# The feed forward of a hybrid step in two phases through DRAM, its first product as seven block products

## The chip, the cores and the metric

The kernel runs on one core of one Trainium2 chip. The metric is device microseconds of one execution; the profile is one execution of the same program, recorded by the hardware profiler. TensorE (PE) multiplies matrices, VectorE (DVE) and ScalarE (ACT) do elementwise work and read PE's result banks, GpSimd (POOL) does small elementwise work and issues DMA transfers, SyncE (SP) issues DMA transfers.

## The reference, cut to what matters

```python
D_MODEL, D_FF, SEQ, DEC_SEQ = 1024, 4096, 128, 2048
# layer, same weights for 128 context and 2048 latent tokens
mix = concatenate([o_a, o_b, o_c], axis=-1) @ w_out
x = x + gate1 * mix
h = rmsnorm(x, norm2_g) * (1 + scale2) + shift2
x = x + gate2 * (square(relu(h @ w_ff1)) @ w_ff2)
y = rmsnorm(x, final_g)
```

w_out is 1024 x 1024, w_ff1 is 1024 x 4096, w_ff2 is 4096 x 1024, all fp32. The 2176 tokens are 17 tiles of 128: tile 0 holds the context, tiles 1 to 16 the latents.

## The kernel before, in words

Every product of fp32 operands is made of three matmuls: each operand is split into a high part (a rounding copy, ACT) and a low part (the operand less the high part, DVE or POOL), and mm3 adds high x high, high x low and low x high. A matmul takes 128 rows of contraction, 128 rows of output and up to 512 columns.

Three parts run one after the other: the attention and convolution groups, the output projection (its first rounding copy at 709 us) and the feed forward (from 944 us).

The output projection (out_proj, L752) goes through the tiles from 16 down to 0, 48 matmuls of 512 columns each. For a tile, the concatenated groups are loaded (mt, from mix_d), rounded on ACT (L771, hi) and subtracted on POOL (L772, lo). When its products are done, `done` applies gate and residual on DVE (L780, L781), stores x1 (L783, POOL's queue), squares on ACT, and gets the norm's factor by DVE (L156), POOL (L157) and ACT (L787). Four transposes per half and four ACT activations then give h2; these steps (h2_half) are woven into the next tile's products, behind 12 of its 16 units and behind the last. h2 is split and kept in SBUF for tiles 8 to 0, and stored to DRAM for 16 to 9.

The feed forward takes the tiles in two groups, GA (8 to 0) and GB (16 to 9). For a group it goes through 16 chunks of two feature tiles; in a chunk, through blocks of three tiles. ff1 makes z for a block (384 columns, 256 in GB's last block; 16 units of 3 matmuls), ACT applies relu, DVE squares and splits (L1194, L168). ff2 multiplies with w_ff2, 512 columns at a time, and DVE adds each result bank to a tile's sum in SBUF (L1222). GA's last chunk applies gate, residual and last norm woven between GB's first units; for GB, the gate is in w_ff2 already (L1259) and the residual starts the sum. The second group loads its h2 at the switch by POOL (L1284). Each group loads and splits both weights anew.

PE runs in the order of the code. The order of the instructions on ACT, DVE, POOL and SP is set by a scheduler when the kernel is built; each of them runs its list in order and stops at an instruction whose semaphore is not there.

## Time and profile before

| | |
|---|---|
| time, 3 runs | 2467.24, 2467.26 and 2470.92 us, median 2467.26 |
| profiled execution, first to last instruction | 2465.8 us |
| PE busy | 2405.0 us, 98% |
| DVE, ACT, POOL busy | 1505.7, 852.7 and 370.4 us |
| DMA | 259.30 MB, mean 105 GB/s |

The profiled execution's span leaves about 1.5 us of the runs' median to what lies around it. A row of the page has an engine's busy time; the time line has single instructions and the idle time in front of them with the instruction that ended it; the groups by line have mean durations. L lines are those of the kernel before. PE's matmul rows have modelled ends that overlap the next row's start, so a matmul's pace is read from the starts of two neighbouring rows.

### The profile page before, as it was taken

How to read it: one execution, taken by the hardware profiler on the slowest of the kernel's cores; microseconds unless marked ns; L12 is line 12 of the kernel's file. 1: busy time of each engine (PE TensorE's matmuls, PEld its weight loads, DVE VectorE, ACT ScalarE, POOL GpSimd, SP SyncE). 2: the span in 40 equal slices, each digit the busy share in tenths (PEclk: the TensorE clock that was granted, in tenths of full speed). 3: DMA queues.
4: the chain of work that ended last, by engine and by line, in shares of the span. 5: the costliest groups of instructions: out<-in, count | busy, mean ns of one | idle time of the engine just before them, and what ended most of it. 6: DMA issues, size and time to landing. Idle time of an engine off the chain costs nothing.

```text
span 2465.8 us, 34981 instructions
## 1 busy us (share of the span) xinstructions
PE 2405.0 (98%) x13906; PEld 2106.4 (85%) x13906; DVE 1505.7 (61%) x2674; ACT 852.7 (35%) x1792; POOL 370.4 (15%) x469
## 2 busy tenths in 40 slices
PE   7999999999999999999999999999999999999998
PEld 5788887777777878999999999999899999999997
DVE  5887845877888865444444444445955555545555
ACT  4666664333346675221212121212322222212212
POOL 2332325444424330000000000002100000000000
PEclk9999999999999999999999999999999999999999
DMA  8655635333354543111111111118821111111101
GB/s 284 230 198 197 220 107 182 122 127 126 126 178 172 207 164 120 43 50 36 52 35 41 46 46 41 35 52 154 263 81 42 51 52 52 38 48 52 52 18 69
DMA packets 162547, 259.30 MB, mean 105 GB/s; under 512 B 10597, under 2 KB 103055, under 8 KB 157776
## 3 DMA queue, kind: packets, MB, share of 16 engines
q1 hardware_dynamic: 128304, 172.86, 22.4%
q0 software_dynamic: 34080, 84.21, 10.6%
q8 instruction: 109, 1.79, 0.3%
q14 instruction: 54, 0.44, 0.1%
HBM read 188.07 MB, written 68.96 MB: 104 GB/s over the span
## 4 chain that ended last, share of the span: by engine, by line
PE 66%; DVE 12%; issue 4%; POOL 3%; ACT 3%; DMA 1%; POOLq 0%; DVEq 0%; SPq 0%; ACTq 0%
PE z L122 35%; PE g L122 30%; DVE cacc L69 6%; DVE uv L69 1%; POOL mv L157 1%; PE g L125 1%; DVE w L781 1%; DVE w L69 1%; POOL s L157 1%; DVE w L1222 0%; ACT w L66 0%; DVE w L168 0%; ACT osq L1056 0%; POOL ssq L157 0%; ACT uv L66 0%
## 5 line engine op out<-in xcount | busy, mean ns | idle before, releaser
L122 PE MATMUL g<-w,xp 128*128 128x512 f32 x3264 | 761.3, 391 | 4.3 <-DVE w L1222 4.3
L122 PEld LDWEIGHTS g<-w,xp 128*128 128x128 f32 x3264 | 611.3, 188 | 129.3 <-DVE w L1222 5.6
L122 PE MATMUL z<-w,hb 128*128 128x512 f32 (+1 forms) x3062 | 704.5, 377 | 4.6 <-ACT w L167 2.3
L122 PEld LDWEIGHTS z<-w,hb 128*128 128x128 f32 x3062 | 524.6, 190 | 105.0 <-issue 4.8
L122 PE MATMUL z<-ab,w 128*128 128x384 f32 x3072 | 544.8, 335 | 0.0
L122 PEld LDWEIGHTS z<-ab,w 128*128 128x128 f32 x3072 | 535.8, 188 | 4.9
L1222 DVE TENSOR_TENSOR w<-g,w 128x512 f32<-128x512 f32 x526 | 360.5, 690 | 191.8 <-PE g L122 190.5
L66 ACT ACTIVATE rl<-z 128x384 f32<-128x384 f32 (+1 forms) x192 | 90.5, 472 | 706.4 <-PE z L122 706.4
L1194 DVE TENSOR_TENSOR rl<-rl 128x384 f32<-128x384 f32 (+1 forms) x192 | 102.6, 534 | 342.0 <-ACT rl L66 342.0
L167 ACT CAST w<-raw 128x1024 fp32r<-128x1024 f32 x148 | 151.7, 1048 | 312.3 <-PE z L122 160.7
L168 DVE TENSOR_TENSOR w<-raw,w 128x1024 fp32r<-128x1024 f32 x147 | 179.8, 1235 | 122.1 <-ACT w L167 87.9
L122 PE MATMUL z<-h2c,w 128*128 128x384 f32 (+1 forms) x1536 | 232.1, 311 | 0.0
L122 PEld LDWEIGHTS z<-h2c,w 128*128 128x128 f32 x1536 | 229.4, 188 | 2.5
L69 DVE SCALAR_TENSOR_TENSOR cacc<-xp,wd,cacc 128x512 f32<-128x512 f32 (+2 forms) x360 | 231.3, 694 | 0.0
L157 POOL TENSOR_TENSOR ssq<-ssq,mhalf 128x1 f32<-128x1 f32 x51 | 38.5, 756 | 746.6 <-DVE ssq L156 738.7
L167 ACT CAST xp<-rl 128x384 fp32r<-128x384 f32 (+1 forms) x192 | 95.2, 496 | 128.0 <-DVE rl L1194 125.5
L168 DVE TENSOR_TENSOR xp<-rl,xp 128x384 fp32r<-128x384 f32 (+1 forms) x192 | 102.3, 533 | 51.8 <-ACT xp L167 51.8
L1284 POOL DMA_DIRECT2D ab<-h_d x12 | 10.6, 901 | 754.2 <-PE z L122 754.2
L69 DVE SCALAR_TENSOR_TENSOR cacc<-raw,sc,cacc 128x512 f32<-128x512 f32 x112 | 85.0, 796 | 0.3
L66 ACT ACTIVATE hc<-g,sh,s 128x128 f32<-128x128 f32 x128 | 50.3, 457 | 39.9 <-PE g L125 22.9
L66 ACT ACTIVATE w<-g,modc,s 128x128 f32<-128x128 f32 x136 | 51.8, 460 | 18.5 <-PE g L125 18.5
L1032 POOL TENSOR_TENSOR r<-fs,r 64x512 f32<-64x512 f32 x31 | 43.8, 1412 | 3.1 <-DMA r<-ss_d 0.7
(228 smaller groups left out, 1804.7 us busy)
## 6 DMA issues: line engine op xcount, KB each, us to landing
raw<-in_w_ff_dram SPq DMA_DIRECT2D x128, 512.0 KB
raw<-in_w_mod_dram SPq DMA_DIRECT2D x32, 512.0 KB
hb<-hT_d POOLq DMA_DIRECT2D x15, 1024.0 KB, 5.8
hT_d<-hb POOLq DMA_DIRECT2D x13, 1024.0 KB, 7.0
ss_d<-ss POOLq DMA_DIRECT2D x34, 256.0 KB, 4.0
r<-ss_d SPq DMA_DIRECT2D x34, 256.0 KB
x_d<-w POOLq DMA_DIRECT2D x17, 512.0 KB, 4.4
out_dram<-w SPq DMA_DIRECT2D x34, 256.0 KB
```

The costliest lines, as they stand in the source:

```text
L66: return S.activation(out=out, in_=in_, func=func, scale=scale, bias=bias, **kw)
L69: return V.scalar_tensor_tensor(out=out, in0=in0, scalar=scalar, in1=in1, op0=op0, op1=op1)
L122: tc.keep_in_program_order(T.matmul(out, lhsT, rhs, start=start, stop=stop))
L125: tc.keep_in_program_order(T.transpose(out, in_, ident if idn is None else idn))
L157: G.tensor_tensor(out=out, in0=out, in1=mhalf[:, 0:out.shape[-1]], op=ALU.pow)
L167: order(S.copy(out=hi, in_=src))
L168: order(V.tensor_tensor(out=lo, in0=src, in1=hi.bitcast(F32), op=ALU.subtract))
L781: V.tensor_tensor(out=x1[:, fs], in0=tmp[:, fs], in1=x1[:, fs], op=ALU.add)
L1032: G.tensor_tensor(out=r[64:128].rearrange("p (h v) -> p h v", h=H), in0=f, in1=r[64:128].rearrange("p (h v) -> p h v", h=H), op=ALU.add)
L1194: V.tensor_tensor(out=rl[:, 0:n], in0=rl[:, 0:n], in1=rl[:, 0:n], op=ALU.mult)
L1222: V.tensor_tensor(out=y[:, hs], in0=py, in1=y[:, hs], op=ALU.add)
L1284: st.dma_start(out=h2[1, b][a][:, :, jj * P:(jj + 1) * P], in_=h2_d[grp[3 * b + jj]][:, a])
```

## The change

The feed forward is no longer taken in chunks of both products. First h @ w_ff1 is made for all tokens and its squared relu stored to DRAM (f_d); then the second product runs over all 17 tiles in one pass.

For the first product the latent tiles are two groups g of eight (16 to 9, 8 to 1). A group's activations and a pair of feature tiles form a 2 x 2 by 2 x 2 block product: contraction halves of 512, token halves (even and odd tiles, 4 tiles, 512 columns), two feature tiles. It is made with seven block products and sums (Strassen, in Winograd's form) instead of eight. A unit (g, i), of which there are 32, is 7 products of 4 contraction tiles of 3 matmuls, 84 matmuls of 512 columns. Four of the products share result bank za, two zc, one gb; ACT and DVE read the partial sums on the way (ff1_units, `after`). The four left operands beside the plain weights come from four DVE sums per unit, and are split; the weights are loaded per unit, once for each g. The seven right operands come from h2: out_proj makes them per pair of an even and an odd tile with four DVE subtractions (h2_pair) and stores them to tb_d; 14 blocks of 512 KB per group are loaded back on POOL's queue (L1176) and split in place on ACT and DVE (L1169, L1170). The context tile has its own 24 matmuls of 256 columns per feature pair, beside g = 0.

For the second product, 8 chunks of four feature tiles; in each, blocks of four tiles and one block with the context. It has the same 3264 matmuls of 512 columns. F is reloaded (SP) and split in place, w_ff2 is loaded once. The first chunk is copied out by ACT, the other seven added by DVE (L1405). The last chunk applies gate, residual, square and last norm to each tile (finish, L1372 to L1376, L160, L161).

In out_proj, tiles below 16 take their loaded and split inputs from a new pool (T, 18 buffers), which later holds right operands and the sums. Its code is otherwise as before; lines are shifted (L771 is L767 now, L772 is L768, L780 is L777, L783 is L780, L787 is L784, L157 is L161).

```diff
         cq.finish(t)
-        if t > 2:
+        if t == NT - 1:
             hu, mt = hunit()
             mh, ml = hu[:, 0], hu[:, 1]
         else:
-            # the units hold the last block of the feed forward by now
-            mt, mh = raw(), xp_tile()[:, 0:D].bitcast(F32R)
-            ml = wtile() if t == 1 else xp_tile()[:, 0:D].bitcast(F32R)
+            mt, mh, ml = tunit(F32), tunit(), tunit()
         ld.dma_start(out=mt, in_=mix_d[t].rearrange("p k t -> p (k t)"))
         S.copy(out=mh, in_=mt)
         G.tensor_tensor(out=ml, in0=mt, in1=mh.bitcast(F32), op=ALU.subtract)
         x1 = wtile(F32)
...
+            if t == 0:
+                split(hc[0][:, ks], hc[1][:, ks], hf[:, ks])
+            elif kq == 1:
+                h2_pair(t, hf)
         return units, [(12, lambda: h2_half(0)), (16, lambda: h2_half(1))]
+    def h2_pair(t, hf):
+        g, j = (NT - 1 - t) // 8, (NT - 1 - t) % 8 // 2
+        js = slice(j * P, (j + 1) * P)
+        dst = tb_d[g]
+        if t % 2 == 0:
+            keep[0] = hf
+            st.dma_start(out=dst[:, 0:2, :, js], in_=hf.rearrange("p (i k) t -> p i k t", i=2))
+            return
+        b11, b21, b12, b22 = keep[0][:, 0:4], keep[0][:, 4:8], hf[:, 0:4], hf[:, 4:8]
+        cb = [tunit(F32).rearrange("p (i k t) -> p i k t", i=2, k=4) for _ in range(2)]
+        V.tensor_tensor(out=cb[0][:, 1], in0=b12, in1=b11, op=ALU.subtract)
+        V.tensor_tensor(out=cb[0][:, 0], in0=b22, in1=cb[0][:, 1], op=ALU.subtract)
+        V.tensor_tensor(out=cb[1][:, 0], in0=b22, in1=b12, op=ALU.subtract)
+        V.tensor_tensor(out=cb[1][:, 1], in0=b21, in1=cb[0][:, 0], op=ALU.subtract)
+        st.dma_start(out=dst[:, 5, :, js], in_=b22)
+        st.dma_start(out=dst[:, 2:4, :, js], in_=cb[0])
+        for i in range(2):
+            st.dma_start(out=dst[:, 4 + 2 * i, :, js], in_=cb[1][:, i])
...
+    hbs.close()
+    tp.append(tps.enter_context(tc.tile_pool(name="tp", bufs=1, side="right", reuse_waits="tile")))
+    hc = []
     for t in range(NT - 2, -1, -1):
         units, nxt_late = out_proj(t)
-        items = late3 + ticks(16, RATE3)
         if t == 0:
-            items.append((4, lambda: load_ff1(0, 0)))
-        weave(units, items)
+            hc += [tunit().rearrange("p (k t) -> p k t", k=KD) for _ in range(2)]
+        weave(units, late3 + ticks(16, RATE3))
         late3 = nxt_late
+    wps.close()
...
+    def split_in_place(hi, lo):
+        S.copy(out=hi, in_=lo.bitcast(F32))
+        V.tensor_tensor(out=lo, in0=lo.bitcast(F32), in1=hi.bitcast(F32), op=ALU.subtract)
+    def right_operand(g, i, kk, dst):
+        unit = tunit if i < 4 else uunit
+        hi, lo = unit(), unit()
+        st.dma_start(out=lo.bitcast(F32).rearrange("p (k n) -> p k n", k=2), in_=tb_d[g][:, i, 2 * kk:2 * kk + 2])
+        split_in_place(hi, lo)
+        dst[i, kk] = (hi, lo)
...
+            a1, a2 = (rw[x].rearrange("p (k f n) -> p k f n", k=4, f=2) for x in range(2))
+            sf[r] = cacc()
+            s_ = sf[r].rearrange("p (k f n) -> p k f n", k=4, f=2)
+            if r == 0:
+                V.tensor_tensor(out=s_[:, :, 0], in0=a1[:, :, 1], in1=a2[:, :, 1], op=ALU.add)
+                V.tensor_tensor(out=s_[:, :, 1], in0=s_[:, :, 0], in1=a1[:, :, 0], op=ALU.subtract)
+            else:
+                s2_ = sf[0].rearrange("p (k f n) -> p k f n", k=4, f=2)[:, :, 1]
+                V.tensor_tensor(out=s_[:, :, 0], in0=a1[:, :, 0], in1=a1[:, :, 1], op=ALU.subtract)
+                V.tensor_tensor(out=s_[:, :, 1], in0=a2[:, :, 0], in1=s2_, op=ALU.subtract)
+        def mixed(r):
+            hi, lo = wunit(), wunit()
+            split(hi, lo, sf[r])
+            w[2 + r] = [x.rearrange("p (k f n) -> p k f n", k=4, f=2) for x in (hi, lo)]
+        return w, [lambda: load(0), lambda: load(1), lambda: plain(0), lambda: plain(1),
+                   lambda: sums(0), lambda: mixed(0), lambda: sums(1), lambda: mixed(1)]
...
+    LEFT = ((0, 0), (1, 0), (2, 1), (2, 0), (3, 0), (3, 1), (1, 1))
+    def ff1_units(g, i, w, tb):
+        za, zc, gb = zbank(), zbank(), gbank()
+        f0, f1 = xp_tile()[:, 0:D], xp_tile()[:, 0:D]
+        left, right = slice(0, 512), slice(512, 1024)
+        bank = (za, gb, za, zc, za, zc, za)
+        def square(x):
+            stt(x, x, 0.0, x, ALU.max, ALU.mult)
+        def after(p):
+            if p == 0:
+                S.copy(out=f0[:, left], in_=za)
+            elif p == 1:
+                V.tensor_tensor(out=f0[:, left], in0=f0[:, left], in1=gb, op=ALU.add)
+                square(f0[:, left])
+            elif p == 2:
+                S.copy(out=f0[:, right], in_=za)
+            elif p == 3:
+                S.copy(out=f1[:, right], in_=zc)
+            elif p == 4:
+                V.tensor_tensor(out=f1[:, right], in0=f1[:, right], in1=za, op=ALU.add)
+                square(f1[:, right])
+            elif p == 5:
+                V.tensor_tensor(out=f0[:, right], in0=f0[:, right], in1=zc, op=ALU.add)
+                square(f0[:, right])
+                st.dma_start(out=f_d[i][g][:, 0], in_=f0)
+            else:
+                act(f1[:, left], za, AF.Relu)
+                V.tensor_tensor(out=f1[:, left], in0=f1[:, left], in1=f1[:, left], op=ALU.mult)
+                st.dma_start(out=f_d[i][g][:, 1], in_=f1)
+        def unit(p, k):
+            r, f = LEFT[p]
+            th, tl = tb[p, k // 2]
+            ks = slice(k % 2 * 512, (k % 2 + 1) * 512)
+            mm3(bank[p], w[r][0][:, k, f], w[r][1][:, k, f], th[:, ks], tl[:, ks],
+                k == 0 and p in (0, 1, 3), k == 3, p != 1)
+            if k == 3:
+                after(p)
+        return [lambda p=p, k=k: unit(p, k) for p in range(7) for k in range(4)]
...
+    TB = [{}, {}]
+    ORDER = [(i, kk) for i in range(7) for kk in range(2)]
+    w, steps = left_operand(0)
...
+        f()
+    for i, kk in ORDER[8:]:
+        right_operand(0, i, kk, TB[0])
...
+    turn = None
+    w2_first = []
+    for g in range(2):
+        for i in range(NP):
+            units = ff1_units(g, i, w, TB[g])
...
+                items += [(12, late3[0][1]), (20, late3[1][1])]
+            if (g, i) != (1, NP - 1):
+                w, steps = left_operand((i + 1) % NP)
+                items += zip((0, 0.5, 5.5, 10.5, 13.5, 17.5, 18.5, 25.5), steps)
+            if (g, i) == (0, NP - 1):
+                items += [(4 * p + 4.5 + kk, lambda p=p, kk=kk: right_operand(1, p, kk, TB[1])) for p, kk in ORDER]
...
+    def load_f(c, b):
+        out = []
+        def step(p):
+            i = c * CF // 2 + p
+            hi, lo = uunit(), uunit()
+            n = 512 if b < 4 else P
+            lv = lo[:, 0:2 * n]
+            src_ = f_d[i][b // 2][:, :, b % 2 * 512:b % 2 * 512 + 512] if b < 4 else fc_d[i]
+            ld.dma_start(out=lv.bitcast(F32).rearrange("p (f n) -> p f n", f=2), in_=src_)
+            split_in_place(hi[:, 0:2 * n], lv)
+            out.append([x[:, 0:2 * n].rearrange("p (f n) -> p f n", f=2) for x in (hi, lo)])
...
+                mm3(py, fh[:, f % 2, js], fl[:, f % 2, js], w2[f][0][:, hs], w2[f][1][:, hs], f == 0, f == CF - 1)
+                if f < CF - 1:
+                    return
+                if c == 0:
+                    if h == 0:
+                        ya[t] = tunit(F32)
+                    S.copy(out=ya[t][:, hs], in_=py)
+                else:
+                    V.tensor_tensor(out=ya[t][:, hs], in0=py, in1=ya[t][:, hs], op=ALU.add)
+                if c == NC_ - 1:
+                    if h == 0:
+                        fin.append(finish(t, ya[t]))
+                    fin[0](h)
...
+        w2n = []
+        for b in range(5):
+            units = ff2_units(c, b, F, w2)
+            items = []
+            nb, ncx = (b + 1, c) if b < 4 else (0, c + 1)
+            if ncx < NC_:
+                F, steps = load_f(ncx, nb)
+                items += zip((3.5, 9.5) if b < 4 else (0, 1), steps)
+            if c + 1 < NC_ and b < 4:
+                items.append((14.5, lambda f=(c + 1) * CF + b: w2n.append(load_ff2(f))))
+            weave(units, items)
+        w2 = w2n
+    tps.close()
```

What stands on ACT in the middle of the output projection, before: L787 is a tile's last scaling (tile 10 and 9 here), L771 the rounding copy of a later tile's input (7 and 6).

```order
L787 ACTIVATE w<-w,ssq_8775 128x1024
L66 ACTIVATE w<-g,modc,s_4853 128x128 x4
L167 CAST ab<-w 128x512
L771 CAST hb<-hc 128x1024
L66 ACTIVATE w<-g,modc,s_4853 128x128 x4
L66 ACTIVATE w,ssq_8875<-w 128x1024
L167 CAST ab<-w 128x512
L787 ACTIVATE w<-w,ssq_8875 128x1024
L66 ACTIVATE w<-g,modc,s_4853 128x128 x4
L167 CAST ab<-w 128x512
L771 CAST hb<-hc 128x1024
```

After: L784 is the last scaling of tile 12, 11 and 10, L767 the rounding copies of tiles 11 and 10, then of 9 and 8.

```order
L64 ACTIVATE w<-g,modc,s_4886 128x128
L784 ACTIVATE w<-w,ssq_8604 128x1024
L767 CAST T<-T 128x1024 x2
L64 ACTIVATE w<-g,modc,s_4886 128x128 x7
L64 ACTIVATE w,ssq_8709<-w 128x1024
L64 ACTIVATE w<-g,modc,s_4886 128x128
L784 ACTIVATE w<-w,ssq_8709 128x1024
L64 ACTIVATE w<-g,modc,s_4886 128x128 x7
L64 ACTIVATE w,ssq_8805<-w 128x1024
L64 ACTIVATE w<-g,modc,s_4886 128x128
L784 ACTIVATE w<-w,ssq_8805 128x1024
L767 CAST T<-T 128x1024 x2
```

Before, the copy of tile 7 stands ahead of the scaling of tile 9, so it is taken two tiles before it is needed. Now the copies of an odd tile and of the even one after it stand together, right behind the scaling of the tile before the odd one. This holds for all eight odd tiles, 15 to 1.

POOL around the end of the output projection, before: L783 stores x1 of tiles 2, 1 and 0 (x_d_161 to x_d_159), L1284 loads activations some 760 us later.

```order
L783 DMA x_d_161<-w 128x1024
L157 TENSOR_TENSOR ssq_9686<-ssq_9686,mhalf 128x1
L783 DMA x_d_160<-w 128x1024
L157 TENSOR_TENSOR ssq_9783<-ssq_9783,mhalf 128x1
L783 DMA x_d_159<-w 128x1024
L157 TENSOR_TENSOR ssq_9882<-ssq_9882,mhalf 128x1
L1284 DMA ab<-h_d_193 128x8x128 x2
```

After: L832 and L834 store a pair's right operands (those of tile 3's pair first, then of tile 1's), L768 subtracts for tiles 1 and 0, L780 stores x1, L1176 loads right operands of the first product.

```order
L834 DMA tb_d_178<-T 128x4x128 x2
L768 TENSOR_TENSOR T<-T 128x1024 x2
L780 DMA x_d_160<-w 128x1024
L161 TENSOR_TENSOR ssq_9823<-ssq_9823,mhalf 128x1
L822 DMA tb_d_178<-w 128x8x128
L780 DMA x_d_159<-w 128x1024
L161 TENSOR_TENSOR ssq_9915<-ssq_9915,mhalf 128x1
L831 DMA tb_d_178<-w 128x4x128
L832 DMA tb_d_178<-T 128x8x128
L834 DMA tb_d_178<-T 128x4x128 x2
L1176 DMA T<-tb_d_177 128x1024
L1176 DMA u<-tb_d_177 128x1024
```

The subtractions of an odd tile and the next stand behind the stores of the pair before, and the loads for the first product behind the last pair's stores.

DVE near the end, before: L1222 adds a result bank, L69 is the last scaling, L1147 and L156 belong to the norm.

```order
L156 TENSOR_SCALAR ssq_21121<-ssq_21121 128x1
L1222 TENSOR_TENSOR w<-g,w 128x512
L69 SCALAR_TENSOR_TENSOR w<-w,ssq_21121,cacc 128x512 x2
L1147 TENSOR_TENSOR ssq_21147<-ssq_21147 128x1
L1222 TENSOR_TENSOR w<-g,w 128x512
L156 TENSOR_SCALAR ssq_21147<-ssq_21147 128x1
L1222 TENSOR_TENSOR w<-g,w 128x512
L69 SCALAR_TENSOR_TENSOR w<-w,ssq_21147,cacc 128x512 x2
```

After: L1405 adds a result bank, L1372 and L1373 apply gate and residual, L67 is the last scaling, L1376 and L160 belong to the norm.

```order
L1405 TENSOR_TENSOR T<-z,T 128x512
L1376 TENSOR_TENSOR ssq_19222<-ssq_19222 128x1
L1405 TENSOR_TENSOR T<-g,T 128x512
L160 TENSOR_SCALAR ssq_19222<-ssq_19222 128x1
L1372 TENSOR_TENSOR T<-T,cacc 128x512
L67 SCALAR_TENSOR_TENSOR T<-T,ssq_19222,cacc 128x512 x2
L1373 TENSOR_TENSOR T<-raw,T 128x512
L1372 TENSOR_TENSOR T<-T,cacc 128x512
L1405 TENSOR_TENSOR T<-z,T 128x512
L1373 TENSOR_TENSOR T<-raw,T 128x512
```

Per tile of the last chunk, four operations of 128 x 512 for gate and residual stand beside the two additions and the two scalings.

## Rows read from the trace of the kernel before

**Rows 1.** Page, first part: busy us, share of the span, instructions.
```profile
PE 2405.0 (98%) x13906; PEld 2106.4 (85%) x13906; DVE 1505.7 (61%) x2674; ACT 852.7 (35%) x1792; POOL 370.4 (15%) x469
```

**Rows 2.** Time line of PE: start us, us, engine line operation out<-in, count [idle before <-releaser].
```profile
1608.00 8.36 PE L122 MATMUL g<-w,xp 128*128 128x512 f32 x36
1616.20 8.59 PE L122 MATMUL z<-h2c,w 128*128 128x384 f32 x48
...
1632.80 8.51 PE L122 MATMUL z<-ab,w 128*128 128x384 f32 x48
1641.15 4.06 PE L122 MATMUL g<-w,xp 128*128 128x512 f32 x17
```

**Rows 3.** Time line of PE, last block of the second group, 256 columns.
```profile
2392.77 5.92 PE L122 MATMUL z<-h2c,w 128*128 128x256 f32 x48
2398.52 1.78 PE L122 MATMUL g<-w,xp 128*128 128x512 f32 x7
```

**Rows 4.** Time line, all engines, the last tile of the output projection.
```profile
944.27 0.68 DVE L780 TENSOR_TENSOR w<-z,w 128x512 f32<-128x512 f32 x1
...
944.34 6.50 PE L122 MATMUL z<-ab,w 128*128 128x384 f32 x36
944.62 1.50 ACT L66 ACTIVATE w<-g,modc,s 128x128 f32<-128x128 f32 x4 [0.99 <-PE g L125]
944.99 0.69 DVE L781 TENSOR_TENSOR w<-w 128x512 f32<-128x512 f32 x1
945.98 0.57 POOL L783 DMA_DIRECT2D x_d<-w  x1 [9.93 <-DVE w L781]
946.00 1.07 ACT L66 ACTIVATE w<-w 128x1024 f32<-128x1024 f32 x1
...
947.26 0.15 DVE L156 TENSOR_SCALAR ssq<-ssq 128x1 f32<-128x1 f32 x1 [1.58 <-ACT w L66]
947.51 0.56 POOL L157 TENSOR_TENSOR ssq<-ssq,mhalf 128x1 f32<-128x1 f32 x1 [0.96 <-DVE ssq L156]
...
948.10 1.15 ACT L787 ACTIVATE w<-w,ssq 128x1024 f32<-128x1024 f32 x1 [0.43 <-POOL ssq L157]
```

**Rows 5.** Groups by line and form: the output projection's split; busy us, mean ns.
```profile
L772 POOL TENSOR_TENSOR hb<-hc,hb 128x1024 fp32r<-128x1024 f32 x14 | 36.4, 2602 | 49.4 <-issue 31.6 <-ACT hb L771 17.7
...
L771 ACT CAST hb<-hc 128x1024 fp32r<-128x1024 f32 x14 | 14.8, 1055 | 10.7 <-PE z L122 10.0 <-DMA hc<-mix_d 0.7
```

**Rows 6.** Groups by line and form, VectorE.
```profile
L1222 DVE TENSOR_TENSOR w<-g,w 128x512 f32<-128x512 f32 x526 | 360.5, 690 | 191.8 <-PE g L122 190.5 <-DMA w<-x_d 1.1
...
L168 DVE TENSOR_TENSOR w<-raw,w 128x1024 fp32r<-128x1024 f32 x147 | 179.8, 1235 | 122.1 <-ACT w L167 87.9 <-PE z L122 34.3
```

**Rows 7.** Time line of PE, the switch between the groups of tiles.
```profile
1731.35 3.02 PE L122 MATMUL g<-w,xp 128*128 128x512 f32 x12 [1.72 <-DVE w L1222]
...
1781.62 4.61 PE L122 MATMUL g<-w,xp 128*128 128x512 f32 x12 [2.30 <-DVE w L1222]
1786.07 4.17 PE L122 MATMUL z<-ab,w 128*128 128x384 f32 x23
```

**Rows 8.** Stretches: us, busy of each engine (instructions), granted clock, DMA share, GB/s.
```profile
900.00:944.00 44.00, 44.00 (x209) 36.18 (x208) 22.01 (x31) 30.63 (x59) 9.85 (x10) 1.00 0.52 168
1730.00:1740.00 10.00, 8.65 (x46) 8.15 (x47) 9.54 (x19) 1.40 (x5) 2.34 (x3) 1.00 1.15 353
1782.00:1784.00 2.00, 2.00 (x7) 1.55 (x6) 1.49 (x5) 0.00 (x0) 0.34 (x1) 0.63 1.02 412
```

**Rows 9.** Time line of POOL: loads of the second group's activations.
```profile
1707.67 5.25 POOL L1284 DMA_DIRECT2D ab<-h_d  x6 [11.15 <-PE z L122]
```

**Rows 10.** DMA issues: operation, count, KB each, median us to landing.
```profile
ab<-h_d POOLq DMA_DIRECT2D x12, 512.0 KB, 8.0
```

**Rows 11.** Time line, the end: last products, last scaling.
```profile
2442.86 13.80 PE L122 MATMUL g<-w,xp 128*128 128x512 f32 x60
...
2461.07 1.41 DVE L69 SCALAR_TENSOR_TENSOR w<-w,ssq,cacc 128x512 f32<-128x512 f32 x2 [0.75 <-POOL ssq L157]
```

More of the change, by code (lines that the diff above doesn't have):

```diff
@@ L774, in out_proj @@
         ld.dma_start(out=x1, in_=x_rows(t))
[L775 removed]
+        tmp = xp_tile()[:, 0:D] if t == 0 else wtile(F32)
         def done(half):
@@ L1295, in tile_hybrid @@
-    ff2(*prev)
+        hi, lo = wunit(), wunit()
+        split(hi, lo, rw)
+        return hi, lo
+    def load_f(c, b):
[9 more added lines that the diff above has]
+            out.append([x[:, 0:2 * n].rearrange("p (f n) -> p f n", f=2) for x in (hi, lo)])
+        return out, [lambda p=p: step(p) for p in range(CF // 2)]
```

278 lines of the change are left out of this document (120 added, 158 removed).

## The prediction

> **What bounds the kernel now.** I read the page's busy times first, then PE's time line in the feed forward, then the places where PE waits, then the queues around the places that the change touches. PE is busy 98% of the span [rows 1], and in the feed forward one product follows the other without a wait that the time line shows [rows 2]. So the kernel lasts as long as PE's columns take, and a matmul's pace is the difference between two starts: 36 of 512 columns in 8.20 us, 228 ns each; 48 of 384 in 8.35 us, 174 ns [rows 2]; 48 of 256 in 5.75 us, 120 ns [rows 3]. The output projection keeps PE busy in 44.00 of 44.00 us at the full granted clock while DVE has 22.0 and ACT 30.6 us of work there [rows 8]: neither bounds it, as long as what PE needs is made early.
>
> The feed forward goes from 944.34 us [rows 4] to the last matmul's end, 2442.86 + 13.80 = 2456.7 us [rows 11]: 1512.3 us. Its work is 3840 x 0.174 + 768 x 0.120 + 3264 x 0.228 = 668.2 + 92.0 + 743.5 = 1503.7 us, so 8.6 us are lost, most of it in the waits at the switch of the groups and behind them [rows 7]. The end of the span lies 9.1 us behind the last matmul.
>
> **The change part by part. Columns.** First product: 32 x 84 = 2688 matmuls x 0.228 = 612.3 us, the context's 16 x 24 = 384 x 0.120 = 46.0, 32 transposes of 128 columns at 0.06 to 0.12 each, 2.8. Second product as before, 743.5. Sum 1404.6: 99.1 us less. The 8.6 us lost go too and are replaced by the waits below.
>
> **Within a unit of the first product** PE takes 19.1 us. DVE has 4 splits x 1.235 + 11 operations x 0.69 [rows 6], 12.5 us. Each product lasts 2.73 us, and between the end of one that uses a bank and the next that writes the same bank another product runs: it covers an ACT copy or a DVE addition of 0.69 us. I count no wait; if the cover went, it would be a rival (below). The 2 x 512 KB stored and 2 x 512 KB loaded per unit are some 110 GB/s, against 353 and 412 GB/s seen [rows 8].
>
> **Output projection: the added wait.** The code looks alike, but the order puts the rounding copy of each odd tile (15 to 1) behind the last scaling of the tile before it on ACT, and that scaling needs that tile's last matmul. PE's first matmul of the odd tile needs the copy. So PE waits through the chain that rows 4 show for the last tile, where nothing waited for it. Matmuls end at about 944; in the order of the chain: DVE 944.27 and 944.99, ACT's square 946.00, DVE 947.26, POOL 947.51, scaling 948.10 + 1.15 = 949.25 [rows 4]. The copy adds 1.055 [rows 5]: PE restarts at 950.3 instead of 944.34, 6.0 us late. Then POOL's subtraction, which stands behind the preceding pair's stores and needs the copy, takes 2.60 us [rows 5]; PE has two matmuls (0.46 us) without it and waits 2.2 us more. Queued behind the copy on ACT is the even tile's copy, which comes early enough; behind the subtraction on POOL the even tile's. In two or three of the eight places DVE has the pair's subtractions or a convolution step in front; I add nothing for them. Eight times 8.2 is 65.6 us.
>
> The clock: after a wait of 2.30 us PE's 12 matmuls took 4.45 us instead of 2.73, with a granted clock of 0.63 (1.2 GHz for most of that stretch); after one of 1.72 the 12 that followed have 3.02 in their row against 4.61 [rows 7, 8]. Behind 6.0 us I expect the former, 1.7 us, each time: 13.6 us. Together 79 us, 9.9 per odd tile. Lower end: 6.0 each, 48 us (POOL's part hidden, clock kept); upper end 13 each, 104 us (DVE's pair and the stores in front of POOL's subtraction, 2 to 3 us).
>
> **Start of the first product.** POOL issues the right operands' loads behind the last pair's stores. That pair's activations follow the last tile's transposes (ACT 944.62 to 946.1, one behind the square, so 947.6), then three subtractions, 2.1 us, and stores of 0.57 each [rows 4]: the first load goes out some 6.3 us after 944.34. 14 loads are 7.3 MB, 21 us at 353 GB/s [rows 8]; one of six issued together landed 8.0 us after its issue [rows 10], so I count 5 us behind the last bytes' turn, and ACT and DVE need 1.05 + 1.235 us each [rows 5, 6]. The last operand needed for the fourth product is the last loaded, so it is ready after about 36 us; PE has 3.5 products, 9.6 us, to do till then. Wait 26.5, with the clock 29. Before, PE went on at once [rows 4]. Lower end 17 (412 GB/s, landing at once), upper end 38 (DVE's 19 splits, 23.5 us, begun when half of the loads have landed).
>
> On the loads the Trainium skill speaks against the change: "SBUF — State Buffer" (section "SBUF: two separate sides") says that a transfer issued by GpSimd waits for its descriptors while VectorE holds the port that both share, and gives about 3.1 us instead of 0.62 for one. The row: six such loads were issued in 5.25 us, 0.88 each [rows 9], beside a DVE busy for most of it. By the row the issue of 14 takes 12 us, less than the transfer; the rule is a rival below.
>
> **Switch of the first product's groups.** The second 14 operands can be loaded only as the first ones' buffers come free, and DVE has 14 x 1.235 = 17.3 us of splits beside the units' 12.5 each: 42 us of work in two units of 19.1 and the context's 2.9. The operands of the third and fourth product come last; by DVE's order they are about 6.8 us late, 8.5 with the clock. Before, this switch cost 1.72 + 2.30 and 1.7 [rows 7]; ends 0 and 17.
>
> **Into the second product** the first chunk's F blocks and weights are split in the last unit's shadow but for one pair: 3 us (0 to 6).
>
> **Seven chunk boundaries.** 11 buffers hold 8 for the chunk and 3 of the next; the rest of the next chunk's splits run in the last 2 us of the chunk, three DVE subtractions of 1.235 in a row. I take 2.5 for the first and 0.5 for each other, 5.5; ends 0 and 7 x 3.7 = 26.
>
> **The last chunk** has the epilogue of all 17 tiles. DVE per tile: 2 x 0.69 to add, 4 x 0.69 for gate and residual, 2 x 0.15, and 1.41 for the scalings [rows 4, 6, 11]: 5.84; PE needs 24 x 0.228 = 5.47. With the F splits left, 8.2 us, DVE has 107.5 and starts 2.9 us behind the chunk's first matmul; PE has 93.0. The norm, store and end add 5.2: 115.6, so the end lies 22.6 us behind PE's ideal end instead of 9.1: 13.5 us more (10 to 18).
>
> **Sum.** -99.1 - 8.6 + 79 + 29 + 8.5 + 3 + 5.5 + 13.5 = +30.8. From the profiled execution's span of 2465.8 that is 2496.6; the median lies 1.5 us above the span, so 2498 us.
>
> **The rivals.**
> *Not slower: the eight waits cost at most 6 us each.* Place: the first and third matmul of the odd tiles. It decides at 79 - 31 = 48 us, 6.0 each. For it: a wait of 1.72 us left the clock up [rows 7], and POOL's subtraction might start with less delay. Against: 6.0 is what the chain takes without POOL and clock. At 48 the time is 2467, and each microsecond per wait less gives 8: at 4.5 us each it is 2455.
> *Dearer stalls.* DVE's queue in front of the chain, chunk boundaries at 2.5 us each and the upper end of the start: + 12 + 14 + 9 = 2533. For it: DVE is at 95% in the switch of before [rows 8], and such a state gave all its waits.
> *The start runs at the rule's price.* Loads issued 3.1 us apart instead of 0.88: the last goes out 40 us behind the first instead of 12, and the end of the loads moves by some 17; four stores per pair in the projection come later too, some 2 us for each of seven: 2530. Against it the row above.
> *Each unit's last product waits for DVE's addition* (the queue behind a split that waits for weights): 2.3 us and 1.7 for the clock in 32 units, 128 us, 2626.
> *The feed forward's own stalls are small:* start 20, switch 4, boundaries and entry 2, end 10: -23.5, 2474.
>
> **How the numbers follow.** My forecast (2480 to 2520) has 0.55; dearer stalls 0.13, the rule 0.03, units that wait 0.03; small stalls 0.12; not slower 0.14. A difference below 0.2%, 5 us, can't be told from none here. The not slower case gives 0.08 to faster and 0.06 to the same, the small stalls 0.02 to the same; the rest, 0.84, is slower. The range, 2460 to 2535, leaves out the lowest part of the not slower case and units that wait.
>
> **What would show it.** In the output projection PE must be idle eight times for about 6 us ended by ACT's copy and 2 us ended by POOL's subtraction, one tile in two, with a low granted clock behind it; its stage grows by some 80 us. The feed forward, from the projection's last matmul to its own last, must take 1450 to 1465 us. PE waits 25 us or more around the first units, some us at the sixteenth, DVE is without a gap in the last 100 us. I am wrong if the odd tiles start without waits, or if DVE's additions hold PE in each unit.

## The result, and the profile after

The changed kernel takes 2514.2 us (median of 4 runs, 2510.7 to 2517.5) against 2469.1 us (2467.2 to 2471.0) for the kernel before on the same chip: 1.0183 times as long, 95% interval 1.0169 to 1.0198. The forecast was 2498 us, with a range of 2460 to 2535. The two profiled executions have spans of 2515.1 and 2465.8 us, 49.3 us apart; the sums below are made on these.

The page of the changed kernel, its first part (busy us, share of the span, instructions), answers to [rows 1]:

```profile
PE 2349.2 (93%) x12402; PEld 1921.3 (76%) x12402; DVE 1472.8 (59%) x2492; ACT 890.1 (35%) x1710; POOL 436.8 (17%) x593
```

PE has less to do and is idle for 7% of the span instead of 2. The group of the output projection's matmuls says where most of that is (busy us, mean ns, then idle time and what ended it):

```profile
L126 PE MATMUL z<-w,T 128*128 128x512 f32 x768 | 212.1, 431 | 65.9 <-ACT T L767 51.2 <-POOL T L768 14.7
```

65.9 us of idle time in front of one group that had none worth a line before. PE's time line shows one of the eight places, tile 11 (start, us, what, count, idle time before and what ended it):

```profile
816.79 0.60 PE L129 MATMUL g<-ident,w 128*128 128x128 f32 x4
823.05 1.22 PE L126 MATMUL z<-w,T 128*128 128x512 f32 x2 [5.67 <-ACT T L767]
826.45 10.76 PE L126 MATMUL z<-w,T 128*128 128x512 f32 x34 [2.17 <-POOL T L768]
837.05 0.60 PE L129 MATMUL g<-ident,w 128*128 128x128 f32 x4
```

ACT's rows at that place, where L784 is the last scaling of tile 12 and L767 the rounding copies of tiles 11 and 10:

```profile
820.92 1.15 ACT L784 ACTIVATE w<-w,ssq 128x1024 f32<-128x1024 f32 x1 [0.95 <-POOL ssq L161]
821.97 1.98 ACT L767 CAST T<-T 128x1024 fp32r<-128x1024 f32 x2
```

The copies begin as the scaling ends, without a wait for their load. Two matmuls wait 5.67 us for the first of them, the third 2.17 us more for POOL's subtraction; and then 34 matmuls take 837.05 - 826.45 = 10.60 us, where at 0.228 they would take 7.75. The stretch around it (us, busy time of PE, PEld, DVE, ACT, POOL with instructions, granted clock, DMA share, GB/s) has a granted clock of 0.84, a mean of time at its two levels of 2.4 and 1.2 GHz, where [rows 8] had 1.00; that is the 2.85 us:

```profile
825.00:860.00 35.00, 27.70 (x112) 21.70 (x112) 23.34 (x31) 12.28 (x24) 11.26 (x12) 0.84 0.39 138
```

Against the end at 944.34 us [rows 4] the projection ends at 1030.44 + 0.60 = 1031.0 (first row below): 86.7 us later, of which 65.9 us are idle time in front of this group. The other 20.8 are a remainder and not the clock alone. PE came 2.0 us later into this part than in the kernel before (its last matmul that reads `wlast`, ahead of the projection, starts at 726.50 instead of 724.46 us), and the 8.9 us for which PE stood idle in this part before have shrunk to 3.0. What is left, 86.7 - 2.0 - (65.9 + 3.0 - 8.9) = 24.7 us, is how much longer the same matmuls take, about 3 per odd tile. The feed forward's start follows on PE's time line:

```profile
1030.44 0.60 PE L129 MATMUL g<-ident,w 128*128 128x128 f32 x4
1046.17 0.79 PE L126 MATMUL z<-T,v 128*128 128x512 f32 x1 [15.12 <-ACT T L1169]
1047.43 2.50 PE L126 MATMUL z<-T,v 128*128 128x512 f32 x5 [0.47 <-DVE T L1170]
1052.24 0.79 PE L126 MATMUL z<-T,v 128*128 128x512 f32 x1 [2.31 <-ACT T L1169]
...
1073.65 2.94 PE L126 MATMUL z<-u,v 128*128 128x512 f32 x12
```

PE waits for the first operands, works on half a product, and waits for the next half. ACT's first copy waits for its load, and the DMA engines are full in that stretch (share 1.02, 372 GB/s):

```profile
1045.07 1.04 ACT L1169 CAST T<-T 128x1024 fp32r<-128x1024 f32 x1 [4.98 <-DMA T<-tb_d]
```

```profile
1040.00:1060.00 20.00, 9.94 (x19) 5.71 (x19) 12.95 (x14) 10.03 (x12) 4.71 (x9) 0.50 1.02 372
```

PE's fifth product starts at 1073.65 us; four products are 10.9 us, so the start lost 1073.65 - 1031.0 - 10.9 = 31.7 us. From then on the units run without waits (PE busy 100% from 1074 to 1420 and from 1450 to 1740). The time line answers to [rows 2] with one unit of the second group of tiles, and the three products ahead of it:

```profile
1464.24 8.34 PE L126 MATMUL z<-u,v 128*128 128x512 f32 x36
1472.42 2.96 PE L126 MATMUL z<-T,v 128*128 128x512 f32 x12
1475.21 2.96 PE L126 MATMUL g<-T,v 128*128 128x512 f32 x12
1478.01 5.76 PE L126 MATMUL z<-T,v 128*128 128x512 f32 x24
1483.61 8.34 PE L126 MATMUL z<-u,v 128*128 128x512 f32 x36
1491.78 2.96 PE L126 MATMUL z<-T,v 128*128 128x512 f32 x12
```

84 matmuls from 1472.42 to 1491.78, 19.36 us, no wait. The last part, PE's last row and DVE's rows to the end, answers to [rows 11]:

```profile
2488.67 2.88 PE L126 MATMUL g<-v,u 128*128 128x512 f32 x12
```

```profile
2499.85 0.68 DVE L1405 TENSOR_TENSOR T<-g,T 128x512 f32<-128x512 f32 x1
...
2505.61 1.41 DVE L67 SCALAR_TENSOR_TENSOR T<-T,ssq,cacc 128x512 f32<-128x512 f32 x2 [0.75 <-POOL ssq L161]
```

PE ends at 2488.67 + 2.72 = 2491.4 us. The addition of what it made last stands on DVE 8.5 us later, behind the epilogues of the tiles before, and the span ends 23.7 us behind PE instead of 9.1.

The 49.3 us are therefore: projection +86.7; feed forward 2491.4 - 1031.0 = 1460.4 instead of 1512.3, -51.9; tail +14.6.

### The profile page after: what moved, and what is told of

It reads as the page before. It is cut to its first block, busy times and chain, and to the rows that moved or that the text cites. A ratio compares the mean times of both kernels' runs of the same rounds, so it can differ in the third digit from the quotient of the medians.

```text
span 2515.1 us, 32249 instructions
## 1 busy us (share of the span) xinstructions
PE 2349.2 (93%) x12402; PEld 1921.3 (76%) x12402; DVE 1472.8 (59%) x2492; ACT 890.1 (35%) x1710; POOL 436.8 (17%) x593
## 3 DMA queue, kind: packets, MB, share of 16 engines
q0 software_dynamic: 34528, 132.46, 14.6%
## 4 chain that ended last, share of the span: by engine, by line
PE 62%; DVE 12%; issue 5%; POOL 4%; DMA 2%; ACT 2%; POOLq 0%; SPq 0%; DVEq 0%; ACTq 0%
PE z L126 42%; PE g L126 19%; DVE cacc L67 5%; DMA u<-tb_d 1%; PE g L129 1%; DVE T L67 1%; POOL T L768 1%; DMA u<-f_d 1%; POOL ssq L161 1%; DVE uv L67 1%; DVE T L1373 1%; POOL mv L161 1%; POOL s L161 1%; DVE T L1405 1%; DVE T L1372 0%
## 5 line engine op out<-in xcount | busy, mean ns | idle before, releaser
L126 PE MATMUL z<-v,u 128*128 128x512 f32 x1632 | 395.0, 391 | 3.5 <-DVE v L172 1.5
L126 PE MATMUL g<-v,u 128*128 128x512 f32 x1632 | 393.6, 391 | 0.0
L126 PEld LDWEIGHTS z<-v,u 128*128 128x128 f32 x1632 | 306.7, 188 | 69.4 <-DVE v L172 2.3
L126 PEld LDWEIGHTS g<-v,u 128*128 128x128 f32 x1632 | 307.7, 189 | 64.0
L126 PE MATMUL z<-T,v 128*128 128x512 f32 x1152 | 286.6, 401 | 29.2 <-ACT T L1169 22.7
L126 PEld LDWEIGHTS z<-T,v 128*128 128x128 f32 x1152 | 217.3, 190 | 84.4 <-ACT T L1169 25.3
L126 PE MATMUL z<-w,T 128*128 128x512 f32 x768 | 212.1, 431 | 65.9 <-ACT T L767 51.2
L126 PE MATMUL z<-u,v 128*128 128x512 f32 x1152 | 269.2, 392 | 0.0
L1169 ACT CAST u<-u 128x1024 fp32r<-128x1024 f32 (+1 forms) x92 | 86.3, 939 | 489.2 <-DMA u<-f_d 330.1
L126 PEld LDWEIGHTS z<-u,v 128*128 128x128 f32 x1152 | 217.6, 189 | 46.5
L126 PEld LDWEIGHTS z<-w,T 128*128 128x128 f32 x768 | 153.4, 207 | 106.1 <-ACT T L767 53.3
L67 DVE SCALAR_TENSOR_TENSOR cacc<-xp,wd,cacc 128x512 f32<-128x512 f32 (+2 forms) x360 | 233.8, 703 | 0.0
L1405 DVE TENSOR_TENSOR T<-z,T 128x512 f32<-128x512 f32 x119 | 82.2, 690 | 160.8 <-PE z L126 160.7
L161 POOL TENSOR_TENSOR ssq<-ssq,mhalf 128x1 f32<-128x1 f32 x51 | 39.0, 765 | 767.8 <-DVE ssq L160 752.4
L1405 DVE TENSOR_TENSOR T<-g,T 128x512 f32<-128x512 f32 x119 | 82.1, 690 | 151.3 <-PE g L126 151.3
L1170 DVE TENSOR_TENSOR u<-u 128x1024 fp32r<-128x1024 f32 (+1 forms) x92 | 99.6, 1082 | 104.8 <-ACT u L1169 104.7
```

What stands on the lines that cost most here:

```text
L67: return V.scalar_tensor_tensor(out=out, in0=in0, scalar=scalar, in1=in1, op0=op0, op1=op1)
L126: tc.keep_in_program_order(T.matmul(out, lhsT, rhs, start=start, stop=stop, skip_group_check=read))
L161: G.tensor_tensor(out=out, in0=out, in1=mhalf[:, 0:out.shape[-1]], op=ALU.pow)
L1169: S.copy(out=hi, in_=lo.bitcast(F32))
L1170: V.tensor_tensor(out=lo, in0=lo.bitcast(F32), in1=hi.bitcast(F32), op=ALU.subtract)
L1405: V.tensor_tensor(out=ya[t][:, hs], in0=py, in1=ya[t][:, hs], op=ALU.add)
```

## The experiments

All ran beside the kernel before, whose median was 2468.0 to 2469.7 us each time. Unless said otherwise, gains are against the changed kernel's 2514.2 us; it ran for the result only, and its four runs lie 6.8 us apart, so a gain or loss of a few us says nothing by itself.

**Copies one tile ahead.** Theory: the eight waits and their clock are the 86.7 us. The edit calls the projection's load, high copy and POOL subtraction before the weave of the preceding tile:

```
...
+        if t > 0:
+            prelude(t - 1)
         weave(units, late3 + ticks(16, RATE3))
```

> Only the place of a few instructions differs from the changed kernel: the load of a tile's mixed input, its high copy on ACT and its POOL subtraction are called one tile ahead in the second output projection, so that on ACT an odd tile's copy stands ahead of the even tile's closing scaling, for tiles 13 to 1; tile 15, for which the pool opens, keeps its wait. Theory (the 82 us that the projection gained are the eight waits for that copy and the clock that they cost): seven of eight waits go, so seven eighths of the 86.7 us by which the projection grew, 76 us, give 2438 us, about 1.2% faster than the kernel before. Rival 1 (the wait moves to the next thing in line, the even tile's copy or the POOL subtraction): the projection keeps 30 to 60 us, 2470 to 2495 us. Rival 2 (only the idle time counts and the clock is lost anyway, because the tiles' matmuls run slowly for another reason): 7/8 of 65.9 us, 2456 us.

Measured: 2445.7 us (2444.6 to 2449.2), 0.9907 of the kernel before (0.9891 to 0.9924): a little faster than the kernel before, by a few steps called one tile earlier. The group, and the new wait of that trace:

```profile
L126 PE MATMUL z<-w,T 128*128 128x512 f32 x768 | 197.6, 411 | 7.1 <-ACT T L764 5.8 <-POOL T L765 1.2
L129 PE MATMUL g<-ident,w 128*128 128x128 f32 x128 | 19.9, 279 | 6.1 <-ACT w L792 6.1
```

65.9 us of idle time became 7.1, all in tile 15. The projection ends 64.6 us earlier than in the changed kernel, not 76: 6.1 us of wait moved to the transposes behind ACT's scaling and took some clock with them (granted 0.95 from 825 to 860 us). The first rival had expected such a move, but to another place (the even tile's copy or POOL's subtraction) and at least five times as large. The second rival (only idle time counts) forecast 2456 and is excluded: matmul time fell from 212.1 to 197.6 us as well.

**Matmuls in the waits.** This prices the clock alone: matmuls whose result nobody reads fill the waits.

```
+        if t % 2 == 1:
+            spare = gbank()
+
+            def keep_warm(n):
+                for _ in range(n):
+                    mm(spare, wo[0][0][0][:, 0:P], wo[0][0][0][:, 0:512])
+
+            keep_warm(24)
+            pad.append(keep_warm)
...
         mm(ps, lh, rl, False, False, read)
+        if pad:
+            pad.pop()(8)
         mm(ps, ll, rh, False, last, read)
```

> In the second output projection 24 matmuls that nobody reads (5.5 us at the pace of the rest) stand before each odd tile's first matmul and 8 more (1.8 us) before its first matmul with the low part: the waits stay, but TensorE works through most of them. Theory (beside the 8.2 us of idle time each wait costs 2.6 us because the granted clock falls to between 0.82 and 0.89 after it): the clock stays at full, and 8 x 2.6 = 21 us come back, 2493 us. Rival 1 (the dummy work itself holds up the matmuls behind it, since some waits are shorter than it): 2505 to 2520 us. Rival 2 (the slow pace of these tiles is not the clock's): 2512 to 2516 us.

Measured: 2499.2 us (2498.2 to 2502.0), -15.0. Tile 11 again (the rows with g<-w are the added ones):

```profile
814.56 5.71 PE L126 MATMUL g<-w 128*128 128x512 f32 x24
820.48 0.72 PE L126 MATMUL z<-w,T 128*128 128x512 f32 x2 [0.21 <-ACT T L771]
821.04 2.00 PE L126 MATMUL g<-w 128*128 128x512 f32 x8
823.91 8.19 PE L126 MATMUL z<-w,T 128*128 128x512 f32 x34 [0.87 <-POOL T L772]
831.94 0.60 PE L129 MATMUL g<-ident,w 128*128 128x128 f32 x4
```

The same 34 matmuls now take 831.94 - 823.91 = 8.03 us instead of 10.60; the granted clock of 825 to 860 us is 1.00 instead of 0.84. So the clock cost these 34 matmuls 2.6 us. Over the eight odd tiles the matmuls behind the waits take 15.6 us less, 1.4 to 2.6 per tile. The two matmuls between the waits can give nothing back, since the wait for POOL takes up what they save; in tile 13 (granted 0.95 from 755 to 790 us) the 8 added matmuls came out 1.5 us later than the wait that they filled, and in tile 5 ACT's copy came 1.0 us later.

**Operands' loads on SP's queue.** Only the queue of one DMA line changes:

```
-        st.dma_start(out=lo.bitcast(F32).rearrange("p (k n) -> p k n", k=2), in_=tb_d[g][:, i, 2 * kk:2 * kk + 2])
+        ld.dma_start(out=lo.bitcast(F32).rearrange("p (k n) -> p k n", k=2), in_=tb_d[g][:, i, 2 * kk:2 * kk + 2])
```

> The loads of the feed forward's right operands (line 1176) are issued from SP's queue, not from POOL's, where they stand behind the last tile's stores. Theory (the first product waits because its load can't be issued before 1037.31 us, six us after the projection ends, and for the rest of the 31 us that the start loses it waits on the transfers and copies of 3.5 MB): 3 to 8 us less than the changed kernel, 2506 to 2511 us, with the first feed-forward matmul some 6 us earlier. Rival 1 (a POOL-issued load is itself dear beside a busy DVE, so all 32 of them slow the start): 17 to 31 us less, 2483 to 2497 us. Rival 2 (what is late is ACT, which has no copies to make before the last tile's own): no change, 2512 to 2516 us.

Measured: 2500.1 us (2496.6 to 2500.3), -14.1, between the theory and its first rival. At the start the theory was about right: the first product's first matmul starts 7.0 us earlier, at 1039.13 instead of 1046.17 us, and the context's matmuls of the first unit at 1079.47 instead of 1082.32, so the start gave 2.9. The last three products of a unit of the second group start at 1452.34 us, in the changed kernel at 1464.24:

```profile
1452.34 8.34 PE L126 MATMUL z<-u,v 128*128 128x512 f32 x36
```

That is 11.9 by then, so 9 came at the switch of the groups, of which the theory said nothing. POOL's time line there, changed kernel:

```profile
1424.94 0.54 POOL L1245 DMA_DIRECT2D f_d<-xp  x1 [8.23 <-DVE xp L67]
1425.47 0.53 POOL L1176 DMA_DIRECT2D u<-tb_d  x1
1425.99 0.53 POOL L1176 DMA_DIRECT2D T<-tb_d  x1
...
1431.07 0.53 POOL L1176 DMA_DIRECT2D u<-tb_d  x1
```

and SP's with the edit:

```profile
1416.20 1.60 SPq L1176 DMA_DIRECT2D u<-tb_d  x2
```

POOL waits 8.23 us to store what DVE has not finished, and the loads stand behind that store. On SP's queue the last of these loads had gone out by 1417.8 us; on POOL's one goes at 1431.07. An issue takes 0.53 us on POOL, and most single ones on SP at that place 0.32 to 0.74, so the issue itself is not dear: it is the order in the queue. The Trainium skill, "SBUF — State Buffer" (section "SBUF: two separate sides"), gives about 3.1 us instead of 0.62 for a transfer issued by GpSimd, and ties this to VectorE instructions in a mode that takes both ports. That price does not show here; DVE is busy in both stretches, for the most part with TENSOR_TENSOR; whether any of its instructions there runs in such a mode no run shows.

**The gate on POOL.** For the tail: the multiplication by the gate, two of six halves per tile that DVE has there.

```
-            V.tensor_tensor(out=y[:, fs], in0=y[:, fs], in1=g2c[:, fs], op=ALU.mult)
+            G.tensor_tensor(out=y[:, fs], in0=y[:, fs], in1=g2c[:, fs], op=ALU.mult)
```

> The multiplication by the gate at the end of the second feed-forward product (line 1372) goes from DVE to POOL. Theory (in the last stretch, after 2400 us, DVE has more to do per tile than PE and falls behind, so that 23.7 us of tail stand behind the last matmul): DVE's work there falls below PE's, the tail falls to 8 to 13 us, and the kernel takes 2500 to 2505 us. Rival (the tail is the chain of one tile's epilogue, not a backlog): POOL's slower multiply is in that chain, and the kernel takes 2514 to 2520 us.

Measured: 2539.5 us (2539.0 to 2540.7), 25 us slower; the theory fails, and the rival too, by 20 us. DVE's time line, one half tile after the other:

```profile
2500.69 0.68 DVE L1405 TENSOR_TENSOR T<-g,T 128x512 f32<-128x512 f32 x1
2502.75 0.69 DVE L1373 TENSOR_TENSOR T<-raw,T 128x512 f32<-128x512 f32 x1 [1.38 <-POOL T L1372]
2503.36 0.68 DVE L1405 TENSOR_TENSOR T<-z,T 128x512 f32<-128x512 f32 x1
2504.23 1.17 DVE L1376 TENSOR_TENSOR ssq<-ssq 128x1 f32<-128x1 f32 x1 [0.19 <-ACT raw L64]
...
2508.28 0.69 DVE L1405 TENSOR_TENSOR T<-g,T 128x512 f32<-128x512 f32 x1
```

DVE's next instruction needs what POOL has just been given, so DVE stands for 1.4 us in each tile, and 0.76 more until POOL has taken the norm's root; the small sum in line 1376 takes 1.17 us beside POOL's multiplication instead of 0.16; and a tile takes 2508.28 - 2500.69 = 7.6 us against PE's 5.44. The rival was right that POOL's multiplication gets into the chain of a tile, and far too low on what it costs.

**The last scaling on ACT and POOL.** Nothing on DVE needs this result:

```
+                    if t == 0:
+                        stt(y[:, fs], y[:, fs], ssq[:, 0:1], fgr[:, fs], ALU.mult, ALU.mult)
+                    else:
+                        S.mul(y[:, fs], y[:, fs], ssq[:, 0:1])
+                        G.tensor_tensor(out=y[:, fs], in0=y[:, fs], in1=fgr[:, fs], op=ALU.mult)
```

> The final scaling of the second feed-forward product (line 1380, two DVE instructions of some 0.7 us in each tile) becomes, for all tiles but the last, a scaling on ACT and a multiplication on POOL; nothing on DVE waits for either. Theory (DVE is a backlog: busy without a pause from before PE's last matmul at 2491.4 to 2507 us, because its work for a tile is a little over PE's 5.44 us): DVE falls to some 4.2 us per tile, the backlog of about 10 us goes, the tail falls from 23.7 to about 14 us, and the kernel takes 2503 to 2507 us. Rival (a chain over three engines with in-order queues sets the pace of a tile, as it did with the gate on POOL): 2514 to 2540 us.

Measured: 2516.5 us (2516.3 to 2523.7), no gain where 10 us were forecast. DVE's additions with both inputs in SBUF, first from 2400 us on in the changed kernel, then in this one, as groups (busy us, mean ns):

```profile
L1373 DVE TENSOR_TENSOR T<-raw,T 128x512 f32<-128x512 f32 x34 | 23.1, 685 | 0.1
```

```profile
L1373 DVE TENSOR_TENSOR T<-raw,T 128x512 f32<-128x512 f32 x34 | 39.2, 1152 | 0.6
L1409 DVE TENSOR_TENSOR T<-z,T 128x512 f32<-128x512 f32 x17 | 11.5, 679 | 0.1
```

The second half's addition, which runs beside POOL's multiplication, takes 1.66 to 1.74 us in 15 of the 17 tiles; the addition with one input in PSUM stays at 0.68. The scalings left 22.6 us of DVE's time free (24.0 to 1.4 in their group), and 16.1 of them went to this neighbour. DVE still needs 2493.77 - 2488.18 = 5.59 us for a tile, by the starts of two of its L1409 rows, against PE's 5.44, so the backlog stays. This profile is of the slowest of the four runs; the trace of the three edits together, below, has the same 39.2 us and 1153 ns. "SBUF — State Buffer" (section "Who interferes with whom") of the Trainium skill says that a DVE instruction with two SBUF inputs and a GpSimd one that reads SBUF contend. This trace agrees, in which additions are slowed (0.69 to some 1.7 us) and which is not (0.68); no run tests the port apart from the rest.

**The join a chunk earlier.** The same tail by less work in the last chunk instead of work moved to another engine: gate and residual are applied to the running sum in the chunk before the last, where DVE is busy 42% (2300 to 2400 us).

```
-                if c == NC_ - 1:
-                    if h == 0:
-                        fin.append(finish(t, ya[t]))
-                    fin[0](h)
+                if c >= NC_ - 2 and h == 0:
+                    fin.append((join if c == NC_ - 2 else finish)(t, ya[t]))
+                if c >= NC_ - 2:
+                    fin[0](*((h,) if c == NC_ - 2 else (h, py)))
...
+            kp(V.tensor_tensor(out=tmp[:, fs], in0=py, in1=g2c[:, fs], op=ALU.mult))
+            kp(V.tensor_tensor(out=y[:, fs], in0=tmp[:, fs], in1=y[:, fs], op=ALU.add))
```

> The last stretch with less work on DVE and none of it on POOL: the gate and the residual are applied to the running sum one chunk earlier, where DVE is busy for 42% of the time, so that the last chunk has four DVE instructions of 0.6 us in a tile in place of six, and a tile's root and scaling stand behind the next tile's halves, so that DVE waits for neither ACT nor POOL. Theory (the tail of 23.7 us holds a backlog of DVE of about 10 us): DVE needs 4.0 us per tile against PE's 5.44, the tail falls to 13 us, and the kernel takes 2502 to 2506 us. Rival (the earlier chunk, where DVE's work more than doubles, now holds up PE, or the last tile's chain and its output DMA of 8 us are the tail): 2511 to 2518 us.

Measured: 2500.0 us (2497.4 to 2501.8), -14.2. DVE now waits for PE, and its last scaling starts 4.0 us behind PE's end, 2482.82 + 2.72 = 2485.5:

```profile
2485.74 0.69 DVE L1391 TENSOR_TENSOR raw<-g,raw 128x512 f32<-128x512 f32 x1 [1.04 <-PE g L126]
...
2489.50 1.41 DVE L67 SCALAR_TENSOR_TENSOR T<-T,ssq,cacc 128x512 f32<-128x512 f32 x2 [0.76 <-POOL ssq L161]
```

The tail is 2499.0 - 2485.5 = 13.5 us, 10.2 less, as forecast. The spans of the two profiled executions are 16.1 us apart; the other 5.9 lie ahead of 1850 us, in stretches that the edit doesn't touch and that differ by some us between executions. The edit does two things, less work per tile and a root and scaling taken behind the next tile's halves; what each gives was not run apart.

**Buffers swapped.** 12 matmuls of one shape take 2.80 us or 2.73 in the rows of one unit above. Which of the two pools holds the operand is exchanged (T for the last four products, u for the first three):

```
-        unit = tunit if i < 4 else uunit
+        unit = tunit if i >= 3 else uunit
```

> The right operands of the feed forward's products change places: those of the first three products lie in the buffers named u and those of the last four in those named T (the changed kernel has the first four in T). In the changed kernel 12 matmuls that read T take 2.80 us (1472.42 to 1475.21) and 12 that read u take 2.73 (a third of 1464.24 to 1472.42). Theory (the pace follows the place of the operand in SBUF): the first three products take 2.73 us each and the last four 2.80, and the total stays at 2510 to 2518 us. Rival (the pace follows the product, its bank or its left operand): the first four stay at 2.80.

Measured: 2503.1 us (2 runs, 2502.0 and 2504.2). PE's time line, one unit:

```profile
1463.69 2.90 PE L126 MATMUL z<-u,v 128*128 128x512 f32 x12
1466.42 2.88 PE L126 MATMUL g<-u,v 128*128 128x512 f32 x12
1469.14 2.88 PE L126 MATMUL z<-u,v 128*128 128x512 f32 x12
1471.86 11.35 PE L126 MATMUL z<-T,v 128*128 128x512 f32 x48
1483.05 2.90 PE L126 MATMUL z<-u,v 128*128 128x512 f32 x12
```

2.72 us per product from u, 11.19 / 4 = 2.80 from T: the pace goes with the buffers, not with the product. Why the place matters stays open. The total fell by 11 us, which neither theory expected. The context's matmuls of the first unit start 4.1 us earlier here than in the changed kernel (1078.26 for 1082.32) and the second group's units 8.7 us earlier, so most of it lies at the start and the switch. Why the exchange shortens those stays open.

**Together.** The first, the second and the scaling edits at once:

> Three edits at once: the copies called one tile ahead, the right operands' loads on SP's queue, and the final scaling off DVE. Theory (they act in different stretches, so their gains add: 68.5 and 14.4 us as measured, and about 10 for the third): 2421 us, 1.9% faster than the kernel before. Rival (the loads on SP collide with the earlier loads of mixed inputs on the same queue, or the gains overlap): 2430 to 2446 us.

Measured: 2436.1 us (2435.1 to 2437.2). From 2445.7, with -14.1 and +2.3, 2434 would follow: the gains add to within 2 us, and the third was none, which is why the theory's 2421 missed.

**First operands earlier.** As the last, with the first four operands called in the projection's last tile:

```
...
+        first_tb = [(3.5 + 3 * n, lambda i=i, kk=kk: right_operand(0, i, kk, TB[0]))
+                    for n, (i, kk) in enumerate(ORDER[:4])]
```

> As the three edits, and the first four of the feed forward's right operands (those of its first two products) are called inside the last tile of the output projection, so that their loads can start before the projection ends. Theory (the 31 us that the feed forward loses at its start are transfers: 14 loads of 512 KB that could only be issued from then on): the first matmul comes some 7 us earlier and the start loses 20 to 24 us, 2410 to 2415 us. Rival (bandwidth as a whole, about 250 to 280 GB/s in this stretch, sets when the fourth product has its operands): the first product starts earlier but the fourth not, 2419 to 2423 us. Rival 2 (the copies of these operands on ACT hold up the last tiles' chain): 2425 us or more.

Measured: 2424.9 us (2422.9 to 2426.7), 11.3 less than with the three edits, where the theory had 6 to 11; its 2410 to 2415 started from the 2421 that the last run had missed. PE's first rows of the feed forward:

```profile
971.34 5.71 PE L126 MATMUL z<-T,v 128*128 128x512 f32 x12 [6.27 <-ACT v L171]
976.89 2.94 PE L126 MATMUL g<-T,v 128*128 128x512 f32 x12
979.67 2.97 PE L126 MATMUL z<-T,v 128*128 128x512 f32 x12
...
991.27 4.09 PE L126 MATMUL z<-u,v 128*128 128x512 f32 x12
```

The first three products run through. The first one starts only 1.6 us earlier than with the three edits (972.96), not 7: it now waits for a weight's copy. The projection ends at 965.1, the fifth product starts at 991.27: 15.3 us lost, against 27 with the three edits alone. So the start waited for the transfers and the copies right behind them, and those that need not wait for the projection's end can go before it.

**All.** That, with the join in place of the moved scaling:

> The copies called one tile ahead, the right operands' loads on SP with the first four called before the projection ends, and the tail's work joined a chunk earlier in place of the scaling on ACT and POOL. Theory (gains add): 2424.9 us as measured without the last edit, less the 2.4 us that the scaling on POOL cost and the 10 of the tail, 2412 us, 2.3% faster than the kernel before. Rival (the tail doesn't shorten): 2420 to 2426 us.

Measured: 2411.4 us (2409.8 to 2411.7), 0.9770 of the kernel before (0.9756 to 0.9785). That is the 2412 of the theory: here the gains added. PE's last row of the projection and its last row of all:

```profile
964.27 0.60 PE L129 MATMUL g<-ident,w 128*128 128x128 f32 x4
...
2396.07 2.88 PE L126 MATMUL g<-v,u 128*128 128x512 f32 x12
```

In this trace (span 2410.0) the projection ends at 964.9, PE at 2396.07 + 2.72 = 2398.8: against the kernel before +20.5, feed forward 1433.9, -78.4, tail 11.2, +2.1; together -55.8.

## Why the prediction was right

The forecast held: slower, by a saving in columns that the stalls behind it ate. The feed forward took 1460.4 us, inside the 1450 to 1465 that the prediction had named. By its steps:

- **Columns, -99.1 and -8.6.** Right but for the pace. A unit takes 19.36 us where 84 x 0.228 is 19.15, and the second product 2.72 per 12 instead of 2.74. With 1404.6 us of work, a start that lost 16 and a switch of 1.2 us, the last kernel's feed forward took 1433.9: of the 12 us left the slower T operands make 9 (32 units x 4 products x 0.07), the second product's faster pace takes 4 away, and what the entry, the chunk boundaries and the clock take was not worked out further. The saving is real; it shows as soon as the stalls go.
- **Odd tiles, +79.** The mechanism and the place were right, and taking the copies ahead shows the cause. That the idle time agrees to 0.3 us (65.6 forecast, 65.9 measured) is luck in part: the waits for ACT were 51.2 us instead of 48, those for POOL 14.7 instead of 17.6. The clock was the mis-sized term: 13.6 forecast, some 24 measured. I took 1.7 us from one wait of 2.30 [rows 7]; behind 5.3 to 8.6 us for ACT and 1.2 to 2.2 for POOL it is about 3 per tile, and the matmuls in the waits give two thirds of it back.
- **Start, +29.** 31.7 measured. The transfers and the copies behind them set it, as the working said; the earlier loads took 12 us of it away.
- **Switch, +8.5.** The size was right (the loads on SP gave 9), the cause only in part: I put it on DVE's splits. DVE had as many splits with the loads on SP's queue, and PE's idle time there was 1.5 us instead of 6.6; what went is the wait of the loads behind POOL's stores. The splits still had a hand in it: the square that the 8.23 us wait was for stood behind two of them on DVE, 1.23 us each. I had named POOL's queue for the start only, and should have written out what stands in front of the second group's loads too.
- **Entry, +3, and chunk boundaries, +5.5.** Entry 2.0 of waits and some clock; boundaries about 1.5 (PE busy 638.5 of 640 us from 1760 to 2400): DVE's three splits there had cover.
- **Last chunk, +13.5.** 14.6, and the backlog is shown by the join. DVE was not without a gap, as the prediction had it: it was busy for 84.05 of the last 91.4 us before PE's end, with waits of up to 0.44 us in each tile for POOL's part of the norm. I took DVE's 5.84 us per tile against PE's 5.47 as a sum of instructions; moving one to POOL, which that sum would recommend, cost 25 us in one run and gained nothing in the other.

Of the rivals, "not slower" fails on the measured 10.8 us per odd tile, "dearer stalls" on the boundaries, the price of POOL's issues on 0.53 us each, "units that wait" on units without a wait, and the small stalls of the feed forward on a start of 31.7 us where they had 20. The sum came 18.5 us short: 7.7 in the projection, 9.8 in the feed forward (1460.4 for 1450.6), 1.1 in the tail.
